# Copies and their subtractions issued apart, and new delays, in a hybrid attention / recurrence layer kernel

## The chip, the core and the metric

The kernel runs on one core of a Trainium2 chip. The metric is the device time of one execution in microseconds (us); several executions are timed and their median is given. Beside them stands one profiled execution, whose trace shows every instruction on five engines: TensorE (PE, with its weight loads as PEld), VectorE (DVE), ScalarE (ACT), GpSimd (POOL) and SyncE (SP, which here only issues DMA transfers, one after the other).

## What is computed

One decoder layer on 512 tokens of width 1024, all in float32. One input projection of width 5912 feeds two mixers: sparse attention (8 heads in 2 groups, with a compressed, a selected-block and a window branch; with 512 tokens the last two both see all earlier tokens) and a gated linear recurrence (4 heads). Each is multiplied by a SiLU gate and projected back; sigmoid gates merge the two; an output projection and a layer norm on `alpha * x + y @ w_out` follow.

```
h = x @ w_in + b_in
q_a, kv_a, g_nsa, z_a, q_b, f_b, i_b, z_b, gm_a, gm_b = split(h)
o_a = nsa_attention(q_a, kv_a, g_nsa) * silu(z_a)
o_b = rmsnorm(hgrn2(q_b, f_b, i_b)) * norm_g * silu(z_b)
y   = sigmoid(gm_a) * (o_a @ w_branch_a) + sigmoid(gm_b) * (o_b @ w_branch_b)
out = layer_norm(alpha * x + y @ w_out)
```

## The kernel before, in words

**Split products.** Every large float32 product is made of three passes in the rounded format float32r: each operand is split into a high part (a copy that rounds, on ACT) and a low part (the operand minus its high part, on DVE), and hi*hi, hi*lo and lo*hi are summed. `split2` (L169) writes the two instructions one behind the other: ACT's copy is L170, DVE's subtraction L171. It is used on the weights (`split`, L231), keys (L576), queries (L586), values (L339), the attention's probabilities (`values`, L728), both mixers' outputs (`ob`, L492, and `oa`, L783) and the merged `y` (L948).

**The projections.** The columns are taken in tiles of 128, in the order `qb0` to `qb3`, then four `proj_i` tiles, then the list `SEQ` (L39), then 16 gate tiles `ga0 gb0 ... gb7`. `proj` (L276) asks for the load of the weight tile three ahead (`load`, L226, a 512 KB transfer into one of three `wraw` buffers), splits the one two ahead, and makes 24 matmuls of 512 columns (8 row blocks, three passes) into a `pa` bank, of which there are two. The result is then moved out of the bank by ACT with its bias.

**The weave.** Everything between the projections is written by generators that a small scheduler in Python, `_Weave` (L74), moves on. `weave.tick()` is called once for every six projection matmuls (in `proj_v`, twelve shorter ones); it resumes each generator whose delay is over; `yield n` asks for n ticks of delay. The delays stand in the dictionary `D` (L70). `claim` keeps users of the same PSUM banks apart. `drain` runs ticks until no generator is left. A later place in this program means a later place in TensorE's queue and in SP's, which keep the order of the program. On ACT, DVE and GpSimd a planner at compile time, with estimated times of its own, chooses among what it takes for ready; earlier in the program goes first. On the chip every engine then takes its queue in order.

**The attention.** `attn_scores` (L645) walks through six units (a block of 128 queries with one or both branches), the longest first. For each it writes score matmuls, then masks and minima (`masked`, DVE L676) with the exps (ACT L679), then `soften` (L686): the reciprocal sums, the scaling by the gates (ACT L700, DVE L702), and transposes of 32x32 blocks into the tile `big` (DVE L710). 16 transfers on SP (L721) carry `big` into `turn`, which completes the transposition; a unit's transfers need the unit before to have left `turn` (`spent`). `values` then splits each part of `turn` (copy, subtraction) and multiplies it with the values. `attn_sum` (L757) adds the branches, multiplies with the gate (L781) and splits the result as `oa`.

**The recurrence.** `hgrn(h)` (L388) runs once per head; `hgrn_norm` (L462) makes the norm. Its four broadcasts (16 transfers) are followed by a product on GpSimd (L488), the gate (L490) and the split into `ob`.

**The end.** Eight branch steps (`BRANCH`, L47, four for mixer b, then four for a, two tiles of `m` each) multiply `ob` and `oa` with the branch weights; L942 and L946 merge, and `y` is split. Meanwhile `out_ahead` (L902) loads the output weights, takes the mean of their rows off (L884, L886) and splits them (L898 on ACT, L899 on DVE). The output product runs over eight row blocks `kt` and needs `y[kt]` and output weight `kt` in turn; its first tile takes both halves of a `kt` together.

Of the kernel before, what the change touches and what calls it, by code (L numbers as in the profile page):

```python
# [18 lines left out]
P = 128  # L19
# [19 lines left out]
SEQ = "kslc q0 kwin q1 v q2 q3 kcmp vcmp zb0 zb1 zb2 zb3 za0 za1 za2 za3".split()  # L39
# [30 lines left out]
D = dict(h0=6, h2=4, h3=7, h4=0, h5=5, h6=3, n0=6, n1=7, n2=4, c0=1, c1=5, c2=5, c3=4, r0=5, p0=5, p1=5, p2=2, s0=8,  # L70
         s2=5, s3=0, v0=10, v1=8, v2=7, v3=8, e0=4, e1=3, t0=6, t1=5, t2=4, t3=5, t4=1, a5=0)
# [35 lines left out]
def layer_kernel(ctx: ExitStack, tc: tile.TileContext, xT, xn, w0, wi, wf, wv, small, brow, consts,  # L107
# [18 lines left out]
    t2 = ctx.enter_context(tc.tile_pool(name="t2", bufs=57))  # L126
# [45 lines left out]


# [64 lines left out]
    for i in range(3):  # L238
        load(i)
# [32 lines left out]
    split(1)  # L272

    weave = _Weave()

    def proj(name):  # L276
        i = M_INDEX[name]
        load(i + 3)
        split(i + 2)
# [36 lines left out]
    def proj_v():  # L316
        i = M_INDEX["v0"]
        load(i + 3)
        split(i + 2)
        load(i + 4)  # L320
        for tt in range(4):
            c = slice(128 * tt, 128 * tt + 128)
            ps = PA()
            for kt in range(KT):
                if kt % 4 == 0:
                    weave.tick()
                if kt < 6:
                    n = slice(PV * (kt % 3), PV * (kt % 3) + NV)
                    hi, lo = (t[:, n] for t in parts[i + kt // 3])
                else:  # L330
                    hi, lo = vtail[kt - 6]
                T.matmul(ps[:, 0:NV], xh[kt][:, c], hi, start=kt == 0, stop=False)
                T.matmul(ps[:, 0:NV], xh[kt][:, c], lo, start=False, stop=False)
                T.matmul(ps[:, 0:NV], xl[kt][:, c], hi, start=False, stop=kt == KT - 1)
            v = T2(NV)
            tc.keep_in_program_order(V.tensor_tensor(v, ps[:, 0:NV], brv, ALU.add))
            vd = vv[:, tt].rearrange("p b (g c) -> p b g c", c=64)
            v4 = v[:, 0:256].rearrange("p (b g c) -> p b g c", b=2, c=64)
            split2(v4, vd[:, :, 0:4:3], vd[:, :, 1:3])  # L339
            G.tensor_copy(gat[:, tt], v[:, 256:NV])  # L340
            vts.append(vv[:, tt])
        gates()
        split(i + 3)
# [8 lines left out]
    def evac(name):  # L352
        ps, m = proj(name)
        r = T2()
        A.activation(r, ps, AF.Identity, bias=bias(m))
        return r
# [105 lines left out]
    def hgrn_norm():  # L462
# [21 lines left out]
        for h in range(4):  # L484
            while "zb%d" % h not in zs:
                yield 1
            o = osq[h][0]
            G.tensor_tensor(o, o, rms[h], ALU.mult)  # L488
# [3 lines left out]
            split2(o, *ob[h])  # L492
            yield 1
# [63 lines left out]
    def gates():  # L557
        gflat = gat.rearrange("p i c -> p (i c)")
        A.activation(gflat, gflat, AF.Exp, scale=-1.0)
        V.tensor_scalar(gflat, gflat, 1.0, 2.0, ALU.add, ALU.mult)  # L560
# [15 lines left out]
    def keys(br, raw):  # L576
        r, rot = rope(raw)
        yield D["r0"]
        V.tensor_tensor(rot, rot, sinT, ALU.mult)
        V.tensor_tensor(r, r, rot, ALU.add)  # L580
        split2(r, KH[:, br], KL[:, br])
        ready.add("keys%d" % br)
# [3 lines left out]
    def queries(m, q):  # L586
# [4 lines left out]
        QAB[m] = T2(dt=F32R), T2(dt=F32R)  # L591
        split2(r, *QAB[m])
# [93 lines left out]
    def soften(u, ms, ts, den):  # L686
        i, brs = units[u]
        n, nb, nm = 128 * (i + 1), len(brs), len(ms)
        while "gates" not in ready:
            yield 1  # L690
# [4 lines left out]
        for ab in range(2):  # L695
            for z, m in enumerate(ms):
                for x in range(nb):
                    c, h = slice(n * x, n * x + n), (ab * nm + z) * nb + x
                    if z % 2:
                        A.mul(ts[m, ab][:, c], ts[m, ab][:, c], den[:, h:h + 1])  # L700
                    else:
                        V.tensor_scalar(ts[m, ab][:, c], ts[m, ab][:, c], den[:, h:h + 1], None, ALU.mult)  # L702
# [25 lines left out]
    def values(u, st, lo):  # L728
# [3 lines left out]
        split2(lo.bitcast(F32), hi, lo)  # L732
# [24 lines left out]
    def attn_sum():  # L757
# [19 lines left out]
        for m in range(4):  # L777
# [4 lines left out]
            oa[m] = T2(dt=F32R), T2(dt=F32R)  # L782
            split2(r, *oa[m])  # L783
            yield 1
# [37 lines left out]
    def cmp_tile(a, name):  # L822
        ps, m = proj(name)
# [3 lines left out]
        weave.start(cmp_hidden(a, de))  # L827
# [3 lines left out]
    def q_tile(m):  # L831
        qraw.append(evac("q%d" % m))
        weave.start(queries(m, qraw[m]))
# [4 lines left out]
    for name in SEQ:  # L838
        if name[1:] == "cmp":
            cmp_tile("kv".index(name[0]), name)  # L840
            if name[0] == "v":
                weave.start(cmp_kv())
            continue
        if name[0] == "k":
            weave.start(keys(int(name == "kwin"), evac(name)))
            continue
        if name[0] == "q":
            m = int(name[1])
            if m == 0:
                split_vtail()  # L850
            q_tile(m)
            if m == 1:
                weave.start(hgrn_norm(), D["s2"])
            if m == 3:
                weave.start(cmp_scores(), D["s3"])
                weave.start(attn_sum())
            continue
        if name == "v":
            weave.start(attn_scores(), D["s0"])
            proj_v()  # L860
            continue
        ps, m = proj(name)
# [4 lines left out]
        V.scalar_tensor_tensor(z, t, 1.0, z, ALU.add, ALU.mult)  # L867
        zs[name] = z
# [12 lines left out]
    def minus_mean(src, scale=1.0):  # L881
        s = SM(2, "rsum")
        for hf in range(2):
            A.activation(src[hf], src[hf], AF.Identity, scale=scale, accum_out=s[:, hf:hf + 1])  # L884
        nm = SM(1, "nm")
# [3 lines left out]
    wmean = {}  # L889

    def mean_out(kt):
        wmean[kt] = minus_mean(woraw[kt])

    def split_out(kt):
        hl = [(T2(dt=F32R), T2(dt=F32R)) for _ in range(2)]
        nm = wmean[kt]
        for raw, (hi, lo) in zip(woraw[kt], hl):
            A.activation(hi, raw, AF.Identity, bias=nm)  # L898
            V.scalar_tensor_tensor(lo, raw, nm, hi.bitcast(F32), ALU.add, ALU.subtract)  # L899
        wo.append(hl)  # L900

    def out_ahead(n):  # L902
        n += AHEAD
        load_out(n + 2)
        if 0 <= n < 8:
            split_out(n)
        if 0 <= n + 1 < 8:
            mean_out(n + 1)


    gm = {}
    for i in range(8):
        for c in "ab":
            name = "g%s%d" % (c, i)
            ps, m = proj(name)
            gm[name] = T2()
            with tc.issue_after(exps[-1]):
                A.activation(gm[name], ps, AF.Tanh, bias=hbias[:, m:m + 1], scale=0.5)
# [3 lines left out]
    y, rb = [], {}  # L922
    lg, lbn = [T2(), T2()], [T2(), T2()]
    for n, (mix, m0) in enumerate(BRANCH):
        i = len(M_TILES) + n
        load(i + 3)
        split(i + 2)
# [3 lines left out]
        for m in (m0, m0 + 1):  # L931
# [9 lines left out]
            r = T2()  # L941
            V.scalar_tensor_tensor(r, gm["g%s%d" % (mix, m)], 1.0, ps, ALU.add, ALU.mult)  # L942
            if mix == "b":
                rb[m] = r
            else:
                V.tensor_tensor(r, r, rb[m], ALU.add)  # L946
                hl = T2(dt=F32R), T2(dt=F32R)
                split2(r, *hl)  # L948
                y.append(hl)
        out_ahead(n)  # L950
    for hf in range(2):
# [8 lines left out]
    for tt in range(4):  # L960
        for hf in range(2):
            dma(res[tt][hf], xn[128 * tt:128 * tt + 128, 512 * hf:512 * hf + 512])
        nm = minus_mean(res[tt], ALPHA)
# [150 lines left out]
```

## Time and profile before

| | |
|---|---|
| time, median of 3 runs | 426.77 us (426.23 to 586.89) |
| the profiled execution's own time | 427.06 us |
| its span, first to last instruction | 425.2 us |
| TensorE / VectorE / ScalarE / GpSimd busy | 409.8 / 314.8 / 239.2 / 10.1 us |
| granted TensorE clock, mean | 0.994 |
| moved by DMA | 58.05 MB |

Times within the trace count from the span's start. In a row of the timeline stand start, duration, engine, line, operation, tiles, shapes, and in brackets the idle time of the engine just before with the instruction that ended it. A row of the waits reads: engine, tile and line that waited, whom it waited for, us in total, how often, the longest. A row of the windows has the length of the stretch, then the busy time and the number of instructions of PE, PEld, DVE, ACT and POOL, then the granted clock, the busy share of the DMA engines and GB/s. A row of the groups has line, engine, operation, tiles, shapes and count, then busy us in all and mean ns of one, then the idle time just before them.

### The profile page before, as it was taken

The page shows a single profiled execution, that of the slowest core. Times are in us where ns is not written, and L with a number is a line of the kernel's source. Part 1 is how long each engine was busy: PE and PEld are TensorE (multiplying, and loading weights), DVE is VectorE, ACT ScalarE, POOL GpSimd, SP SyncE. Part 2 cuts the span into 40 slices and gives each one's busy share as a digit, 9 for nine tenths or more (in the row PEclk, how much of TensorE's full clock was granted, in tenths as well). Part 3 has the DMA queues.
Part 4 walks back from the last instruction along what each step waited for, and adds up shares of the span by engine and source line. Part 5 has one row for each costly group of instructions (what it writes and reads, how often), then busy time and mean ns, then how long its engine had stood idle before and what let it go on. Part 6 is the DMA issues. An engine that isn't in the chain of part 4 may idle for free.

```text
span 425.2 us, 5979 instructions
## 1 busy us (share of the span) xinstructions
PE 409.8 (96%) x2063; PEld 334.2 (79%) x2063; DVE 314.8 (74%) x636; ACT 239.2 (56%) x469; POOL 10.1 (2%) x22
## 2 busy tenths in 40 slices
PE   9999999999999999979999999999999978999994
PEld 8888888889978687757887787788878856887884
DVE  5925698977485979987699679489766699774493
ACT  4535653544476635783667676578584776528301
POOL 2000000000010220000000000000000000000000
PEclk9999999999999999989999999999999999999999
DMA  7995300324113564804821542723944843026022
GB/s 263 396 387 174 137 0 22 130 76 143 57 49 106 170 202 109 256 2 131 206 109 50 132 168 77 190 81 99 230 167 101 293 142 107 0 72 226 2 100 98
DMA packets 25630, 58.05 MB, mean 137 GB/s; under 512 B 4480, under 2 KB 6400, under 8 KB 25600
## 3 DMA queue, kind: packets, MB, share of 16 engines
q1 hardware_dynamic: 25168, 57.28, 43.1%
q10 hardware_dynamic: 432, 0.39, 0.3%
q8 instruction: 16, 0.26, 0.3%
q14 instruction: 14, 0.11, 0.1%
HBM read 41.93 MB, written 2.10 MB: 104 GB/s over the span
## 4 chain that ended last, share of the span: by engine, by line
PE 78%; DVE 8%; ACT 5%; SPq 4%; DMA 2%; issue 2%; DVEq 0%; ACTq 0%
PE pa L115 51%; PE pso L115 12%; PE pss L115 12%; SPq L122 4%; PE pst L115 2%; DMA wraw<-in_wbr_dram 1%; DVE t L171 1%; DVE big L710 1%; ACT t L170 1%; DVE t L942 1%; DVE wlo L171 1%; ACT whi L170 1%; PE pst L119 1%; ACT t L679 1%; DVE t L899 1%
## 5 line engine op out<-in xcount | busy, mean ns | idle before, releaser
L115 PE MATMUL pa<-t,whi 128*128 128x512 f32 x640 | 201.5, 395 | 4.4 <-DVE t L171 3.0
L115 PEld LDWEIGHTS pa<-t,whi 128*128 128x128 f32 x640 | 118.6, 189 | 34.6 <-DVE t L171 4.3
L115 PE MATMUL pa<-t,wlo 128*128 128x512 f32 x320 | 125.0, 391 | 0.0
L171 DVE TENSOR_TENSOR wlo<-wraw,whi 128x1024 fp32r<-128x1024 f32 x46 | 56.7, 1234 | 23.7 <-ACT whi L170 23.6
L115 PEld LDWEIGHTS pa<-t,wlo 128*128 128x128 f32 x320 | 60.2, 188 | 12.8
L170 ACT CAST whi<-wraw 128x1024 fp32r<-128x1024 f32 x46 | 48.1, 1045 | 30.5 <-PE pa L115 24.1
L679 ACT ACTIVATE t<-t,sm_mn 128x512 f32<-128x512 f32 (+3 forms) x64 | 35.2, 551 | 27.6 <-DVE sm_mn L676 27.6
L115 PE MATMUL pso<-t,t 128*128 128x512 f32 (+2 forms) x158 | 32.8, 342 | 0.0
L115 PE MATMUL pss<-t,t 128*128 128x512 f32 (+2 forms) x158 | 30.6, 324 | 0.0
L171 DVE TENSOR_TENSOR turn<-turn,t 128x1024 fp32r<-128x1024 f32 x20 | 23.6, 1215 | 7.3 <-ACT t L170 7.2
L115 PEld LDWEIGHTS pso<-t,t 128*128 128x128 f32 x158 | 25.2, 189 | 3.7
L115 PE MATMUL pa<-t,t 128*128 128x512 f32 (+1 forms) x104 | 27.2, 366 | 0.0
L710 DVE STREAM_TRANSPOSE big<-t 128x512 f32<-128x512 f32 (+2 forms) x48 | 25.8, 590 | 1.0 <-PE pss L115 1.0
L115 PEld LDWEIGHTS pss<-t,t 128*128 128x128 f32 x158 | 24.0, 190 | 2.9
L170 ACT CAST t<-turn 128x1024 fp32r<-128x1024 f32 x20 | 20.0, 1048 | 3.8 <-DMA turn<-big 3.4
L115 PEld LDWEIGHTS pa<-t,t 128*128 128x128 f32 x104 | 18.3, 188 | 3.1
L170 ACT CAST t<-t 128x512 fp32r<-128x512 f32 (+1 forms) x18 | 10.6, 595 | 17.5 <-DVE t L946 12.7
L115 PE MATMUL pa<-turn,t 128*128 128x512 f32 x64 | 19.9, 389 | 0.0
L115 PE MATMUL pss<-t,whi 128*128 128x512 f32 x64 | 19.8, 390 | 0.0
L115 PE MATMUL pso<-t,vv 128*128 128x512 f32 x40 | 16.8, 421 | 2.1 <-ACT t L170 2.1
L700 ACT ACTIVATE t<-t,sm_dn 128x512 f32<-128x512 f32 (+3 forms) x32 | 16.0, 555 | 3.6 <-DVE sm_dn L694 3.5
L676 DVE CUSTOM_DVE_ANT_0 t<-pss,t 128x512 f32<-128x512 f32 (+3 forms) x32 | 14.0, 483 | 5.2 <-PE pss L115 5.2
(198 smaller groups left out, 569.9 us busy)
## 6 DMA issues: line engine op xcount, KB each, us to landing
wraw<-in_wf_dram SPq DMA_DIRECT2D x38, 512.0 KB, 3.6
turn<-big SPq DMA_DIRECT2D x48, 128.0 KB, 2.4
wraw<-in_wbr_dram SPq DMA_DIRECT2D x8, 512.0 KB, 6.0
t<-in_wout_dram SPq DMA_DIRECT2D x16, 256.0 KB, 4.5
t<-t SPq DMA_DIRECT2D x48, 64.0 KB, 2.0
turn<-big SPq DMA_DIRECT2D x32, 96.0 KB, 2.2
t<-in_wi_dram SPq DMA_DIRECT2D x8, 256.0 KB, 6.0
big<-in_w_dram SPq DMA_DIRECT2D x8, 256.0 KB, 5.7
```

What stands on the lines that cost most here:

```text
L115: return tc.keep_in_program_order(nc.tensor.matmul(*a, **k))
L119: return tc.keep_in_program_order(nc.tensor.transpose(*a, **k))
L122: tc.keep_in_program_order(nc.sync.dma_start(o, i))
L170: A.copy(dst_hi, src)
L171: V.tensor_tensor(dst_lo, src, dst_hi.bitcast(F32), ALU.subtract)
L676: V.tensor_tensor_reduce(out=p[:, c], in0=dsts[m, ab][:, c], in1=amask[:, 512 - n:512], op0=ALU.add, op1=ALU.min, scale=-0.125, scalar=3.0e38,
L679: A.activation(p[:, c], p[:, c], AF.Exp, bias=mn[:, h:h + 1], scale=-1.0, accum_out=den[:, h:h + 1])
L700: A.mul(ts[m, ab][:, c], ts[m, ab][:, c], den[:, h:h + 1])
L710: V.transpose(view[:, :, :, 4 * ab + m], ts[m, ab][:, 0:128 * nst].rearrange("p (c b s) -> p c b s", b=4, s=32))
L899: V.scalar_tensor_tensor(lo, raw, nm, hi.bitcast(F32), ALU.add, ALU.subtract)
L942: V.scalar_tensor_tensor(r, gm["g%s%d" % (mix, m)], 1.0, ps, ALU.add, ALU.mult)
```

## The change

- A new generator `split_steps` writes the copy, waits `D["y"]` = 2 ticks, and writes the subtraction. It takes the place of `split2` for keys, queries, values, probabilities, `ob`, `oa` and `y`.
- Weights are split by the generator `weights`: copy one tick after `proj` of the tile two ahead begins (`w0`), subtraction three ticks later (`w1`). Raw weights get a pool of their own, `come`, with 2 buffers (before: 3); the common pool `t2` has 59 buffers (before: 57).
- Evictions of projection tiles are written by generators that start in the next tick (`x0` = 0), the branch merges one tick later (`x1` = 1), instead of straight behind their matmuls.
- `SEQ` begins with `kcmp kslc v q0`, and `kwin` stands behind the queries. `attn_scores` starts after `q1`, with delay 5.
- `masked` keeps the minima only; the exps open `soften`. The scaling writes DVE's part first, then, two ticks later, ACT's.
- The norm product of `hgrn_norm` moves from GpSimd to DVE.
- The output weights' `split_out` becomes a generator: start after 4 ticks (`o2`), sums, 2 ticks (`o0`), mean, 6 ticks (`o1`), copies, 2 ticks, subtractions.
- All `oa` gates are written in one tick; `branch_a` splits each. Behind the branch steps stands a second `weave.drain()`.
- Most delays in `D` have other values.

```
-SEQ = "kslc q0 kwin q1 v q2 q3 kcmp vcmp zb0 zb1 zb2 zb3 za0 za1 za2 za3".split()
+SEQ = "kcmp kslc v q0 q1 q2 q3 kwin vcmp zb0 zb1 zb2 zb3 za0 za1 za2 za3".split()
-D = dict(h0=6, h2=4, h3=7, h4=0, h5=5, h6=3, n0=6, n1=7, n2=4, c0=1, c1=5, c2=5, c3=4, r0=5, p0=5, p1=5, p2=2, s0=8,
-         s2=5, s3=0, v0=10, v1=8, v2=7, v3=8, e0=4, e1=3, t0=6, t1=5, t2=4, t3=5, t4=1, a5=0)
+D = dict(h0=6, h2=5, h3=14, h4=0, h5=7, h6=8, n0=6, n1=3, n2=4, c0=1, c1=3, c2=4, c3=3, r0=5, p0=5, p1=6, p2=2, s0=5,
+         s2=11, s3=2, v0=10, v1=11, v2=5, v3=9, e0=4, e1=2, t0=5, t1=5, t2=4, t3=2, t4=1, a5=1, y=2, w0=1, w1=3,
+         x0=0, x1=1, e2=0, e3=2, o0=2, o1=6, o2=4)
+    come = ctx.enter_context(tc.tile_pool(name="come", bufs=2))
-    t2 = ctx.enter_context(tc.tile_pool(name="t2", bufs=57))
+    t2 = ctx.enter_context(tc.tile_pool(name="t2", bufs=59))
+    def split_steps(src, dst_hi, dst_lo):
+        A.copy(dst_hi, src)
+        yield D["y"]
+        V.tensor_tensor(dst_lo, src, dst_hi.bitcast(F32), ALU.subtract)
-            raws[i] = strm.tile([P, 1024], F32, name="wraw", tag="wraw")
+            raws[i] = come.tile([P, 1024], F32, name="wraw", tag="wraw")
+    def split_later(i):
+        if i < len(order) and i not in parts:
+            weave.start(weights(i), D["w0"])
+    def weights(i):
+        hi = strm.tile([P, 1024], F32R, name="whi", tag="whi")
+        A.copy(hi, raws[i])
+        yield D["w1"]
+        lo = strm.tile([P, 1024], F32R, name="wlo", tag="wlo")
+        V.tensor_tensor(lo, raws[i], hi.bitcast(F32), ALU.subtract)
+        parts[i] = hi, lo
...
-            G.tensor_tensor(o, o, rms[h], ALU.mult)
-            yield 2
+            V.tensor_tensor(o, o, rms[h], ALU.mult)
...
-                                A.activation(p[:, c], p[:, c], AF.Exp, bias=mn[:, h:h + 1], scale=-1.0,
-                                             accum_out=den[:, h:h + 1])
-                weave.start(soften(u, ms, ts, den), D["e1"])
+                weave.start(soften(u, ms, ts, mn, den), D["e2"])
...
     def split_out(kt):
+        s = row_sums(woraw[kt])
+        yield D["o0"]
+        nm = minus_mean(s)
+        yield D["o1"]
         hl = [(T2(dt=F32R), T2(dt=F32R)) for _ in range(2)]
         for raw, (hi, lo) in zip(woraw[kt], hl):
             A.activation(hi, raw, AF.Identity, bias=nm)
+        yield D["y"]
+        for raw, (hi, lo) in zip(woraw[kt], hl):
             V.scalar_tensor_tensor(lo, raw, nm, hi.bitcast(F32), ALU.add, ALU.subtract)
...
-            split_out(n)
+            weave.start(split_out(n), D["o2"])
...
+    def merge(mix, m, ps):
+        r = T2()
+        V.scalar_tensor_tensor(r, gm["g%s%d" % (mix, m)], 1.0, ps, ALU.add, ALU.mult)
+        if mix == "b":
+            rb[m] = r
+            return
+        V.tensor_tensor(r, r, rb[m], ALU.add)
+        yield D["y"]
+        y[m] = T2(dt=F32R), T2(dt=F32R)
+        yield from split_steps(r, *y[m])
+            weave.start(merge(mix, m, ps), D["x1"])
+    weave.drain()
```

More of the change, by code (lines that the diff above doesn't have):

```diff
@@ L236, in split @@
             parts[i] = hi, lo
-    for i in range(3):
+    def split_later(i):
[8 more added lines that the diff above has]
+        parts[i] = hi, lo
+    for i in range(2):
         load(i)
@@ L272, in layer_kernel @@
     split(1)
+    load(2)
     weave = _Weave()
@@ L278, in proj @@
         load(i + 3)
-        split(i + 2)
+        split_later(i + 2)
         hi, lo = parts[i]
@@ L318, in proj_v @@
         load(i + 3)
-        split(i + 2)
-        load(i + 4)
+        split_later(i + 2)
         for tt in range(4):
@@ L334, in proj_v, with values_of @@
                 T.matmul(ps[:, 0:NV], xl[kt][:, c], hi, start=False, stop=kt == KT - 1)
[L335 to L343, printed above, removed]
+            weave.start(values_of(tt, ps), D["x0"])
+            if tt == 1:
+                load(i + 4)
+                split_later(i + 3)
+        weave.start(gates(), 1)
+    def values_of(tt, ps):
+        v = T2(NV)
+        V.tensor_tensor(v, ps[:, 0:NV], brv, ALU.add)
+        yield D["y"]
+        vd = vv[:, tt].rearrange("p b (g c) -> p b g c", c=64)
+        v4 = v[:, 0:256].rearrange("p (b g c) -> p b g c", b=2, c=64)
+        G.tensor_copy(gat[:, tt], v[:, 256:NV])
+        vts.append(vv[:, tt])
+        yield from split_steps(v4, vd[:, :, 0:4:3], vd[:, :, 1:3])
     def silu_tile(name):
@@ L580, in keys @@
         V.tensor_tensor(r, r, rot, ALU.add)
[L581 removed]
+        yield from split_steps(r, KH[:, br], KL[:, br])
         ready.add("keys%d" % br)
@@ L590, in queries @@
         V.tensor_tensor(r, r, rot, ALU.add)
-        QAB[m] = T2(dt=F32R), T2(dt=F32R)
-        split2(r, *QAB[m])
+        qab = T2(dt=F32R), T2(dt=F32R)
+        yield from split_steps(r, *qab)
+        QAB[m] = qab
     PTc = {}
@@ L694, in soften @@
         V.tensor_tensor(den4, den4, gate[:, :, ms[0]:ms[0] + nm], ALU.mult)
[L695 to L702, printed above, removed]
+        for odd in range(2):
+            for ab in range(2):
+                for z, m in enumerate(ms):
+                    for x in range(nb):
+                        c, h = slice(n * x, n * x + n), (ab * nm + z) * nb + x
+                        if z % 2 == odd:
+                            if odd:
+                                A.mul(ts[m, ab][:, c], ts[m, ab][:, c], den[:, h:h + 1])
+                            else:
+                                V.tensor_scalar(ts[m, ab][:, c], ts[m, ab][:, c], den[:, h:h + 1], None, ALU.mult)
+            if odd == 0:
+                yield D["e3"]
         yield D["t0"]
@@ L781, in attn_sum, with branch_a @@
             V.tensor_tensor(r, r, zs["za%d" % m], ALU.mult)
-            oa[m] = T2(dt=F32R), T2(dt=F32R)
-            split2(r, *oa[m])
-            yield 1
+            weave.start(branch_a(m, r), 1)
+    def branch_a(m, r):
+        oa[m] = T2(dt=F32R), T2(dt=F32R)
+        yield from split_steps(r, *oa[m])
     oa = [None] * 4
@@ L826, in cmp_tile, with q_tile, z_tile @@
                      AF.Identity, bias=bias(m))
-        weave.start(cmp_hidden(a, de))
+        yield from cmp_hidden(a, de)
     qraw = []
-    def q_tile(m):
-        qraw.append(evac("q%d" % m))
-        weave.start(queries(m, qraw[m]))
-    for t in range(4):
-        weave.start(hgrn(t), D["h0"])
-        proj_i(t)
[L838 to L862, printed above, removed]
+    def q_tile(m, ps, b):
+        qraw.append(evac(ps, b))
+        yield from queries(m, qraw[m])
+    def z_tile(name, ps, m):
         z, t = T2(), T2()
@@ L866, in layer_kernel, with k_tile @@
             A.activation(t, ps, AF.Tanh, bias=hbias[:, m:m + 1], scale=0.5)
+        yield D["y"]
         V.scalar_tensor_tensor(z, t, 1.0, z, ALU.add, ALU.mult)
         zs[name] = z
+    def k_tile(br, ps, m):
+        yield from keys(br, evac(ps, m))
+    for t in range(4):
+        weave.start(hgrn(t), D["h0"])
+        proj_i(t)
+    for name, after in zip(SEQ, SEQ[1:] + [""]):
+        if after == "v":
+            split_vtail()
+        if name == "v":
+            proj_v()
+            continue
+        ps, m = proj(name)
+        if name[1:] == "cmp":
+            weave.start(cmp_tile("kv".index(name[0]), ps, m), D["x0"])
+            if name[0] == "v":
+                weave.start(cmp_kv())
+        elif name[0] == "k":
+            weave.start(k_tile(int(name == "kwin"), ps, m), D["x0"])
+        elif name[0] == "q":
+            weave.start(q_tile(int(name[1]), ps, m), D["x0"])
+            if name == "q1":
+                weave.start(hgrn_norm(), D["s2"])
+                weave.start(attn_scores(), D["s0"])
+            if name == "q3":
+                weave.start(cmp_scores(), D["s3"])
+                weave.start(attn_sum())
+        else:
+            weave.start(z_tile(name, ps, m), D["x0"])
     wo, woraw = [], {}
@@ L905, in out_ahead, with gate_tile @@
         if 0 <= n < 8:
-            split_out(n)
-        if 0 <= n + 1 < 8:
-            mean_out(n + 1)
+            weave.start(split_out(n), D["o2"])
     gm = {}
+    def gate_tile(name, ps, m):
+        gm[name] = T2()
+        with tc.issue_after(exps[-1]):
+            A.activation(gm[name], ps, AF.Tanh, bias=hbias[:, m:m + 1], scale=0.5)
+        yield 1
     for i in range(8):
@@ L926, in layer_kernel @@
         load(i + 3)
-        split(i + 2)
+        split_later(i + 2)
+        while i not in parts:
+            weave.tick()
         hi, lo = parts[i]
```

52 lines of the change are left out of this document (24 added, 28 removed).

## The prediction

> **What bounds the kernel now.** I read the page's busy line first, then the waits of TensorE alone, then the stretches around each wait, and last the queues that feed it. The busy line and the first full stretch of the chain say that TensorE is the bound.
>
> ```profile
> PE 409.8 (96%) x2063; PEld 334.2 (79%) x2063; DVE 314.8 (74%) x636; ACT 239.2 (56%) x469; POOL 10.1 (2%) x22
> 358.11 2.72 PE pa L115 x12
> ```
>
> Twelve matmuls take 2.72 us, 0.227 us each from start to start, so a step of six (a tick) takes 1.36 us. The change adds and removes no matmul. All it can win is the time in which TensorE stands; here is that time, in full but for the one wait before the first load (1.1 us):
>
> ```profile
> PE pa L115 <- DVE t L171: 3.0, 3, 1.6
> PE pso L115 <- ACT t L170: 2.1, 1, 2.1
> PE pa L115 <- DVE t L942: 1.4, 1, 1.4
> PE pst L115 <- DVE t L171: 1.0, 1, 1.0
> PE pso L115 <- DVE turn L171: 0.8, 1, 0.8
> PE pst L115 <- ACT t L170: 0.7, 1, 0.7
> ```
>
> They sum to 9.0 us and lie at four places, which the timeline of TensorE shows:
>
> ```profile
> 142.55 0.50 PE L115 MATMUL pst<-kh,t 64*128 64x512 f32 x2 [0.99 <-DVE t L171]
> 186.64 0.51 PE L115 MATMUL pso<-t,vv 128*128 128x512 f32 x1 [2.07 <-ACT t L170]
> 187.90 0.50 PE L115 MATMUL pso<-turn,vv 128*128 128x512 f32 x1 [0.75 <-DVE turn L171]
> 188.52 0.63 PE L115 MATMUL pso<-turn,vv 128*128 128x512 f32 x1
> 188.94 0.63 PE L115 MATMUL pso<-t,vv 128*128 128x512 f32 x1
> 348.50 0.70 PE L115 MATMUL pa<-t,whi 128*128 128x512 f32 x2 [1.38 <-DVE t L942]
> 354.60 0.50 PE L115 MATMUL pa<-t,whi 128*128 128x512 f32 x1 [1.56 <-DVE t L171]
> 384.62 1.92 PE L115 MATMUL pst<-t,t 128*128 128x512 f32 x6 [0.68 <-ACT t L170]
> ```
>
> A matmul is shown as busy for about 0.39 us (the wlo row of the page, below) while the next one starts 0.227 after it, so each wait hides 0.16 more. Place 1, the scores of unit 0 for queries 2 and 3: 0.99 + 0.16 = 1.15. Place 2, the first `values` of unit 0: 2.07 + 0.75 + 0.32 = 3.1, and behind it a slow clock: starts are 0.42 apart instead of 0.227 (188.52 to 188.94), over some seven matmuls 1.4 us; together 4.5. Place 3, the first `a` branch product, which needs `oa`: 1.38 + 3.0 + 4 x 0.16 = 5.0. Place 4, the last `y` in the output product: 0.68 + 0.16 = 0.85. In all 11.5 us. The profiled execution took 427.06 (0.3 above the median 426.77), its span 425.2; with all four gone it would be 427.06 - 11.5 = 415.6.
>
> ```profile
> 187.90:191.50 3.60, 3.60 (x9) 2.74 (x10) 3.60 (x5) 2.47 (x3) 0.00 (x0) 0.57 0.00 0
> 346.70:354.60 7.90, 3.51 (x12) 1.65 (x12) 7.90 (x14) 6.93 (x14) 0.00 (x0) 1.00 0.40 134
> ```
>
> The clock column is 0.57 behind place 2 and 1.00 across place 3, though the latter's pauses are longer in sum. So 1.4 us is a price of place 2 only. The Trainium skill (TensorE: Matmul & The Clock Gate, section "Part 1: The HAM clock gate") has the clock halve only after an idle window of about 3.4 us; here pauses of 2.07 and 0.75 with one matmul between sufficed, and the trace decides. By the page a shortened place 2 would leave no clock cost at all, and my sum below would be about 0.4 lower.
>
> **Part by part.** Instructions on DVE and ACT stand in the planner's order, those on TensorE and SP in the order of the program, which the ticks make. I count ticks from the first of `proj_i`.
>
> *Norm product on DVE.* Four GpSimd products go, four DVE products of 0.69 come (as L946): 2.8 us on DVE.
>
> ```profile
> L488 POOL TENSOR_TENSOR t<-t,t 128x512 f32<-128x512 f32 x4 | 5.6, 1391 | 32.7 <-DMA t<-t 32.7
> L946 DVE TENSOR_TENSOR t<-t,t 128x512 f32<-128x512 f32 x8 | 5.5, 691 | 0.2
> 140.66 1.28 POOL L488 TENSOR_TENSOR t<-t,t 128x512 f32<-128x512 f32 x1 [20.42 <-DMA t<-t]
> 140.72 1.77 DVE L171 TENSOR_TENSOR t<-t,t 128x512 fp32r<-128x512 f32 x1
> 146.95 1.84 DVE L171 TENSOR_TENSOR wlo<-wraw,whi 128x1024 fp32r<-128x1024 f32 x1
> 154.63 1.77 DVE L867 SCALAR_TENSOR_TENSOR t<-t,t 128x512 f32<-128x512 f32 x1
> ```
>
> But three DVE instructions that met these products were held: 1.77, 1.84 and 1.77, where L946 takes 0.69, the mean wlo (a row below) 1.23 and an L899 (below), of L867's kind, 0.75. They lost 1.1 + 0.6 + 1.0 = 2.7, so DVE's total stays. The first of them is the very subtraction that place 1 waits for: without its 1.1, that wait is 0.05. Besides, the queries' scores now come 8 ticks after q3's projection (tick 56 after 48; before 54 after 48), 2.7 us more. Against this stand the subtraction's two ticks of delay (`y`=2) and the first scores at tick 47, the same tick in which q1's subtraction is written. Place 1 gains 1.0 (between 0 and 1.15).
>
> *Unit 0's values.* The 16 `turn` transfers are written at tick 68 in both; the first `values` product moves from tick 78 to 80, and eight compressed-score matmuls (about 0.9 us) go ahead of it: TensorE comes 3.6 us later.
>
> ```profile
> L122 SPq DMA_DIRECT2D turn<-big x16: 512/590/597, 164.3 to 173.8; - x16
> L170 ACT CAST t<-turn x4: 1039/1042/1045, 185.5 to 189.3; 128x1024 fp32r<-128x1024 f32 x4
> DMA to landing us min/median/max: 2.3/2.4/2.7
> ```
>
> The data were there at 173.8 + 2.4 = 176.2, and the copy started at 185.5: it stood 9.3 us behind other work in ACT's order, not behind the transfers. So if the copies stay where they are, 3.6 covers the 3.1 and the clock's 1.4; if the planner moves them along by the same two ticks, nothing is won. The transposes too are written 3 ticks later (66, not 63), with 3 fewer ticks to the transfer. I take 3.4 of the 4.5 (0 to 4.5), since the slack of 9.3 is in ACT's queue, where exps now have a step of their own.
>
> *`oa` and the output weights (place 3).* Before, the output weights' copies and subtractions (L898, L899) are written among the steps that lead to `oa`. Now `split_out` waits 4 + 2 + 6 + 2 = 14 ticks, so that the first subtraction is written at tick 166, and all four `oa` subtractions at tick 163; five ticks before TensorE asks.
>
> ```profile
> 335.67 1.05 ACT L170 CAST whi<-wraw 128x1024 fp32r<-128x1024 f32 x1 [2.25 <-DMA wraw<-in_wbr_dram]
> 338.59 1.19 ACT L747 COPY t<-pso 64x512 f32<-64x512 f32 x2
> 353.86 0.68 DVE L171 TENSOR_TENSOR t<-asum,t 128x512 fp32r<-128x512 f32 x1
> L899 DVE SCALAR_TENSOR_TENSOR t<-t,sm_nm,t 128x512 fp32r<-128x512 f32 x16 | 11.5, 748 | 0.6 <-PE pss L115 0.6
> ```
>
> The last `oa` was ready at 353.86 + 0.68 = 354.54. Between 337 and 354, six L899 (4.5 us) stood ahead of it on DVE, and the ACT copy that starts the chain (338.59) stood behind a weight that came late. That weight follows unit 5's transfers, which wait for the last `values` of unit 4, now at tick 145 instead of 148: 4.1 us earlier. So 4.5 + 2 to 4 against a lack of 5.0: I take 4.2 (2 to 5).
>
> *Place 4, what is deferred.* DVE's work up to the last `y` stays the same, and there is little room:
>
> ```profile
> 323.10:346.70 23.60, 23.60 (x105) 19.51 (x104) 16.20 (x23) 14.56 (x26) 0.00 (x0) 1.00 0.64 205
> 354.60:374.40 19.80, 19.80 (x87) 16.38 (x88) 16.93 (x27) 9.36 (x19) 0.00 (x0) 1.00 0.09 28
> 374.40:385.40 11.00, 10.32 (x46) 7.92 (x44) 8.09 (x13) 4.53 (x7) 0.00 (x0) 1.00 0.45 118
> DVE t L171 <- ACT t L170: 4.9, 7, 0.7
> ```
>
> DVE worked 16.20 + 7.90 + 16.93 + 8.09 = 49.1 of 62.3 us from tick 152 to the last `y`. Without places 3 and 4 there are 56.4 us for them. The first window has 7.4 idle, and the deferral leaves three or four more output weights (2 x 0.75 each, 4.5 to 6) for later. What pays for it are the seven waits of 0.7 between a copy and its subtraction (4.9), which `y`=2 fills. Net between -0.85 and +5; I take +1.3.
>
> *Weights.* The raw ring shrinks from 3 to 2, and the subtraction is written 4 ticks before its use instead of 8. The load, once free to run ahead, now waits for the subtraction of the weight before (12 ticks before use), with all later transfers behind it on SP.
>
> ```profile
> wraw<-in_wf_dram SPq DMA_DIRECT2D x38, 512.0 KB, 3.6
> 318.04 10.01 SPq L122 DMA_DIRECT2D turn<-big  x16
> L170 ACT CAST whi<-wraw 128x1024 fp32r<-128x1024 f32 x46 | 48.1, 1045 | 30.5 <-PE pa L115 24.1
> L171 DVE TENSOR_TENSOR wlo<-wraw,whi 128x1024 fp32r<-128x1024 f32 x46 | 56.7, 1234 | 23.7 <-ACT whi L170 23.6
> L115 PE MATMUL pa<-t,wlo 128*128 128x512 f32 x320 | 125.0, 391 | 0.0
> ```
>
> Behind a block of 16 the way is 10.0 + 3.6 + 1.05 + 1.23 = 15.9 us. Twelve ticks are 16.3 at 1.36, and 21.6 at the attention stretch's mean (348.50 - 186.64 over 90 ticks is 1.8). So it is covered by 0.4 to 5.7 us; if that cover is gone each block costs its lateness. I put 1.0 for all (0 to 15).
>
> *The rest.* Evictions are written in the next tick's first step: two `pa` buffers cover one tile (4 ticks, 5.4 us) against an eviction below 0.7, cost 0. SEQ, the exps split from the minima and the scaling by halves move instructions without adding any; the recurrence's delays spread its DVE work. The drain ahead of the `a` products writes five output weights' steps early and issues nothing on TensorE. Together 0, between -1 and +2; I take +0.3, for the first scores.
>
> **Sum.** 427.06 - 1.0 - 3.4 - 4.2 + 1.3 + 1.0 + 0.3 = 421.06; less the 0.3 by which the profiled run lies above the median: about **420.8**. A measurement of this kernel tells some 2% (8.5 us) from no change.
>
> **Rivals.**
>
> *All four places close.* 415.6 - 0.3 = 415.3. For it: in the queue each late thing is late by order, not by work (9.3 us at place 2), and unit 5's chain comes 4 us sooner. Against: DVE would have to be busy for 49.1 of 56.4 us in a stretch that begins with waits.
>
> *The gain is given back.* The planner, not the program, decides where the copies stand; place 2 stays at 4.5, and what place 3 gains comes back before the last `y`: 427.06 - 1.0 + 0.3 - 0.3, some 426. For it: the planner already put L781 between L899s, so handwritten distance may change little. Against: the seven waits of 0.7 show that it doesn't fill all.
>
> *Slower: loads behind blocks.* With two raw buffers SP stands on a load until DVE has done a subtraction, and the block of 16 behind it starts late; the next weight is then late for TensorE. It decides from 5.7 us of lateness in the attention stretch, 0.4 in a stretch of bare ticks. At 3.3 us over that in five of six blocks: 16.5 us on 420.8, less the 1.0 already put, about 436.3. For it: the blocks take 10 us six times and cannot be passed. Against: while TensorE waits, everything else catches up, and the ticks around blocks are the long ones.
>
> **How the numbers follow.** Forecast 0.42 (its own range 417 to 424.5), all four close 0.26, given back 0.20, slower 0.12. Faster by over 2% means under 418.2: all of the second and a tenth of the first, 0.30. Slower by over 2%, above 435.3: most of the last, 0.10. Within 2%: 0.60. The range reaches from 414 (all closed, and one more short wait) to 430, where the last case and its lead-up are left out.
>
> **What would show it.** Right: the waits of TensorE without the `pst` row from L171 and without a pause above 1 us at unit 0's first values, granted clock 1.0 there; the `oa` subtractions before the L899 of output weights 1 to 4; a wait of 1 to 3 us in the output product's first tile. Wrong: rows in which `pa` waits for whi or wlo, or long SP waits on wlo ahead of a block of 16 (the slower rival); the casts of unit 0's `turn` still 9 us after landing (given back).

## The result, and the profile after

The changed kernel takes 421.52 us (median of 6 runs, 420.13 to 424.28), the kernel before 426.85 (6 runs beside it): a ratio of 0.9883 [0.9849, 0.9918], 5.3 us less. The interval lies clear of no change, although the prediction held that only 2% could be told from it. The 586.89 us among the executions of the kernel before belongs to a slow one and stays out of the ratio. The profiled execution took 421.37, its span 419.6, 5.69 less than the profiled 427.06 of before. The forecast of 420.8 is 0.7 from the median. The busy line of the page and TensorE's waits (in total, times, longest):

```profile
PE 408.2 (97%) x2063; PEld 333.9 (80%) x2063; DVE 312.7 (75%) x640; ACT 239.1 (57%) x469; POOL 4.6 (1%) x18
PE pso L116 <- DVE turn L179: 2.0, 1, 2.0
PE pa L116 <- DVE sm_nm L930: 1.5, 1, 1.5
PE pso L116 <- DVE t L189: 1.0, 1, 1.0
PE pso L116 <- ACT t L177: 0.9, 1, 0.9
PE pa L116 <- DVE t L972: 0.3, 1, 0.3
```

Without the wait of the start (L189) 4.8 us are left of 9.0 (2.03, 1.50, 0.92 and 0.34 in the rows below). With the hidden 0.16 for each of the four it is 5.4, where the prediction counted 11.5 with the slow clock. The difference, 6.1, is 0.4 more than what was measured. Of the old waits only 0.34 is left; the other three rows are new or stand elsewhere.

**Unit 0's first values (place 2): the wait is gone.** The timeline of SP, ACT and TensorE there, and the stretch behind it (the column after the engines is the granted clock):

```profile
166.62 10.18 SPq L123 DMA_DIRECT2D turn<-big  x16
178.79 0.72 ACT L718 ACTIVATE t<-t,sm_mn 128x512 f32<-128x512 f32 x1 [2.54 <-DVE sm_mn L702]
179.52 1.99 ACT L177 CAST t<-turn 128x1024 fp32r<-128x1024 f32 x2
188.19 0.40 PE L116 MATMUL pso<-t,vv 128*128 128x512 f32 x1
188.20:191.80 3.60, 3.60 (x17) 2.93 (x16) 3.60 (x8) 3.59 (x5) 0.00 (x0) 1.00 0.00 0
```

The last transfer lands at about 166.62 + 10.18 + 2.4 = 179.2 (2.4 is the median way to landing); the cast starts 0.3 later, where it started 9.3 later in the kernel before. The planner has put it ahead of three of unit 1's four exps. The product starts 6.7 us after the cast has ended, and the clock stays 1.00.

**Unit 1's first values: a wait that was not there.** SP, ACT and TensorE again:

```profile
203.49 11.79 SPq L123 DMA_DIRECT2D turn<-big  x16
218.31 0.62 ACT L718 ACTIVATE t<-t,sm_mn 128x384 f32<-128x384 f32 x1 [2.54 <-DVE sm_mn L702]
222.36 2.92 ACT L177 CAST t<-turn 128x1024 fp32r<-128x1024 f32 x3
223.44 0.50 PE L116 MATMUL pso<-t,vv 128*128 128x512 f32 x1 [0.92 <-ACT t L177]
225.97 0.50 PE L116 MATMUL pso<-turn,vv 128*128 128x512 f32 x1 [2.03 <-DVE turn L179]
```

The data landed at 203.49 + 11.79 + 2.4 = 217.7, the cast started 4.7 later, behind exps of the next unit that had waited 2.54 for their minima. It is the picture of place 2, one unit on.

**`oa` (place 3) and the products behind it.** ACT, DVE and TensorE:

```profile
340.14 2.43 ACT L177 CAST t<-asum 128x512 fp32r<-128x512 f32 x4 [0.56 <-DVE asum L817]
342.97 2.50 DVE L179 TENSOR_TENSOR t<-asum,t 128x512 fp32r<-128x512 f32 x4
347.70 1.41 DVE L943 SCALAR_TENSOR_TENSOR t<-t,sm_nm,t 128x512 fp32r<-128x512 f32 x2
346.20 0.70 PE L116 MATMUL pa<-t,whi 128*128 128x512 f32 x2 [0.34 <-DVE t L972]
358.04 0.68 DVE L972 SCALAR_TENSOR_TENSOR t<-t,pa 128x512 f32<-128x512 f32 x1
358.87 0.71 PE L116 MATMUL pa<-t,whi 128*128 128x512 f32 x2 [1.50 <-DVE sm_nm L930]
```

All four `oa` are ready at 345.47 (354.54 before), ahead of the first deferred subtraction (L943 at 347.70). What had been put off comes next: between 347.70 and 358.04 DVE works through ten L943 among others, and the merge L972 that frees the bank for the next `a` product stands behind them. The 1.50 is put down to the tiny L930; what frees a bank, though, is the L972 in the row above. It ended at 358.72, 0.15 before TensorE went on; at 346.20 the same way took 0.14 (the L972 there ended at 346.06). Without the deferred work in front of it (experiment 8) the wait is gone. No wait is left in the output product.

### The profile page after: what moved, and what is told of

The parts are those of the page before. It is cut to its first block, busy times and chain, and to the rows that moved or that the text cites. A ratio compares the mean times of both kernels' runs of the same rounds, so it can differ in the third digit from the quotient of the medians.

```text
span 419.6 us, 5940 instructions
## 1 busy us (share of the span) xinstructions
PE 408.2 (97%) x2063; PEld 333.9 (80%) x2063; DVE 312.7 (75%) x640; ACT 239.1 (57%) x469; POOL 4.6 (1%) x18
## 4 chain that ended last, share of the span: by engine, by line
PE 84%; DVE 7%; SPq 3%; ACT 3%; DMA 2%; issue 1%; DVEq 0%; ACTq 0%
PE pa L116 55%; PE pso L116 12%; PE pss L116 12%; PE pst L116 5%; SPq L123 3%; ACT t L718 2%; DMA wraw<-in_wbr_dram 2%; DVE big L746 1%; DVE wlo L254 1%; DVE t L943 1%; PE pst L120 1%; DVE asum L788 1%; DVE t L787 1%; DVE t L179 1%; DVE asum L817 1%
## 5 line engine op out<-in xcount | busy, mean ns | idle before, releaser
L254 DVE TENSOR_TENSOR wlo<-wraw,whi 128x1024 fp32r<-128x1024 f32 x44 | 53.6, 1219 | 31.2 <-ACT whi L251 30.2
L251 ACT CAST whi<-wraw 128x1024 fp32r<-128x1024 f32 x44 | 46.1, 1047 | 29.2 <-PE pa L116 19.7
L116 PEld LDWEIGHTS pso<-t,t 128*128 128x128 f32 x158 | 26.1, 197 | 3.9
L116 PE MATMUL pso<-turn,vv 128*128 128x512 f32 x40 | 16.0, 399 | 2.0 <-DVE turn L179 2.0
L177 ACT CAST t<-t 128x512 fp32r<-128x512 f32 x16 | 9.8, 615 | 13.4 <-DVE t L976 11.4
```

Source lines behind the costliest of these rows:

```text
L116: return tc.keep_in_program_order(nc.tensor.matmul(*a, **k))
L177: A.copy(dst_hi, src)
L251: A.copy(hi, raws[i])
L254: V.tensor_tensor(lo, raws[i], hi.bitcast(F32), ALU.subtract)
```

## The experiments

**1. The weights' ring.** Is the two-buffer ring a cost?

```
-    come = ctx.enter_context(tc.tile_pool(name="come", bufs=2))
-    t2 = ctx.enter_context(tc.tile_pool(name="t2", bufs=59))
+    come = ctx.enter_context(tc.tile_pool(name="come", bufs=3))
+    t2 = ctx.enter_context(tc.tile_pool(name="t2", bufs=57))
```

> The changed kernel with three raw weight buffers again (and 57 common ones, as before). My theory: the SP waits on wlo fall from 85.7 us, unit 1's block of 16 starts up to 1.5 us earlier, but the copies of unit 1 stand behind exps on ACT, so the time falls by no more than 1: 420.5 to 421.5. Rival (the smaller ring costs, as the slower rival had it): 2 to 3 us faster, unit 1's waits of 0.92 and 2.03 gone. The other way, two common buffers fewer hold the output weights: up to 1 slower.

423.39 us, ratio 0.9917 [0.9886, 0.9948]. SP's waits on wlo fell, and TensorE's did not; first the row of the changed kernel, then that with three buffers:

```profile
SPq L123 <- DVE wlo L254: 85.7, 16, 12.3
```

```profile
SPq L123 <- DVE wlo L254: 46.0, 7, 12.4
```

No product of TensorE waits for a weight in either, so SP's waiting is not on its path. The changed kernel does show what the prediction named as a sign of the slower rival, a long wait of SP on wlo ahead of a block of 16: 9.9 us, just ahead of unit 1's (203.49). It cost nothing: with three buffers unit 1's block starts at 202.93, and its waits are the same 0.92 and 2.03. The slower rival is out, and so is the 1.0 of the sum. The kernel with three buffers is 1.9 slower (0.9 in the profiled executions), which is not explained in full. Its trace has a wait of 1.2 for an eviction (at 86.88), which the changed kernel does not have, and a slow clock behind unit 1's pause (0.57 from 226 to 230, where the changed kernel has 1.00); with two common buffers fewer besides, the run does not tell what the third buffer alone is worth.

**2. The norm product on VectorE, alone**, in the kernel before (G to V in L488).

> The kernel before, with the norm product alone moved to DVE. My theory: the subtraction at place 1 is no longer held by GpSimd, the pst wait of 0.99 us falls below 0.2, the rest stays: 0.8 to 1.1 us faster, 425.8. Rival (the queries' transfers are what is late): the pst wait stays near 1 us and the time at 426.8. A third: four more DVE products of 0.69 lengthen place 2, 427.5.

427.03, ratio 1.002 [0.9998, 1.0043]. Place 1's wait fell from 0.99 to 0.52, not to 0.05: the subtraction no longer takes 1.77, but the product now stands ahead of it on DVE.

```profile
141.20 0.69 DVE L488 TENSOR_TENSOR t<-t,t 128x512 f32<-128x512 f32 x1
141.81 0.68 DVE L171 TENSOR_TENSOR t<-t,t 128x512 fp32r<-128x512 f32 x1
142.55 0.50 PE L115 MATMUL pst<-kh,t 64*128 64x512 f32 x2 [0.52 <-DVE t L171]
```

The time did not change; the 0.8 to 1.1 us that were expected did not come.

**3. Unit 0's products two ticks later, alone**, in the kernel before. This was the prediction's ground for place 2.

```
-        yield D["t2"]
+        yield D["t2"] + 2 * (u == 0)
```

> The kernel before, with only unit 0's values products two ticks (2.7 us) later, behind copies at the same place. My theory (two ticks of lead are most of place 2's gain): the waits of 2.07 and 0.75 fall to 0 to 0.6 and the clock behind them stays at 1.0: 3 to 4.5 us faster, 423. Rival (the planner moves the copies along): 2 us of wait remain, 426.

434.45, ratio 1.0186 [1.0142, 1.0231]. TensorE waits more, not less:

```profile
PE pso L115 <- ACT t L170: 5.3, 2, 3.6
PE pso L115 <- DVE turn L171: 2.9, 2, 1.8
```

The planner moved the casts along with their consumer. ACT's rows for unit 0 and unit 1:

```profile
187.97 2.95 ACT L170 CAST t<-turn 128x1024 fp32r<-128x1024 f32 x3
229.48 2.92 ACT L170 CAST t<-turn 128x1024 fp32r<-128x1024 f32 x3
```

Unit 0's first cast starts 2.4 later than the 185.54 of before, although its transfers are no later and its place in the program is the same: two activations of another projection now stand ahead of it. Unit 1's stands behind four exps. Unit 0's wait stays and unit 1's comes up. The rival was right about the copies, and the time is slower than either expected; the ground for 3.4 us of the forecast falls.

**4. Unit 1's products two ticks later**, in the changed kernel (with the drain of experiment 8).

> The changed kernel with ticks until the four oa are written in place of the drain ahead of the a products, and unit 1's values products two ticks later. My theory (the 0.92 and 2.03 us at unit 1's first values are a lack of lead, as place 2 was): both go, the clock stays at 1.0, nothing else moves: 417.5 to 419. Rival (the copies follow, or a later unit comes short by the two ticks): 420.5 to 422.

425.03, ratio 0.9969 [0.9954, 0.9985], against 421.19 for the changed kernel with that drain alone: the same again. Unit 1's first cast starts at 227.02 where it started at 222.23 without the two ticks, and its product still waits 1.71 for it. In all 2.1 and 1.9 us of waiting for casts and subtractions stay at units 1 and later, and 2.1 for a `pa` eviction comes on top.

**5. The pairs of `values` taken apart, alone**, in the kernel before; once with the products two ticks later, once at their old ticks (`yield D["t2"] - 2`).

```
-        split2(lo.bitcast(F32), hi, lo)
+        A.copy(hi, lo.bitcast(F32))
+        yield 2
+        V.tensor_tensor(lo, lo.bitcast(F32), hi.bitcast(F32), ALU.subtract)
         yield D["t2"]
```

> The kernel before with one pair alone taken apart: the cast of `turn` and the subtraction behind it in `values`, two ticks between, and the products therefore two ticks later. Separation theory (what the change wins at unit 0's first values is won by the pair being issued apart): TensorE's waits of 2.1 on the cast and 0.75 on the subtraction shrink to under 1 us together, the clock behind them stays 1.0, and the time is 422 to 424.5. Rival (the planner moves the casts along with whatever is written later, as when the products alone were put two ticks later: 434.45): the wait of about 2 us stays at unit 0 or turns up at unit 1, 427 to 434.

> As the run beside it, but the products keep their ticks: cast, two ticks, subtraction, two ticks, product. Separation theory: 423 to 426, with a smaller wait of TensorE at unit 0's first values than the 2.1 + 0.75 before. Rival (order follows the consumer only): within 1 us of before, the casts of unit 0 still some 9 us after the transfers have landed, or slower because the subtraction now has two ticks instead of four to its product.

438.05, ratio 1.0271 [1.0229, 1.0313], and 428.92, ratio 1.0065 [1.0041, 1.0088]. In the second the first wait is the same and the other one longer (1.7 for 0.75):

```profile
PE pso L115 <- ACT t L732: 2.1, 1, 2.1
PE pso L115 <- DVE turn L734: 1.7, 1, 1.7
```

So separating this pair does not close place 2 either; by itself it loses.

**6. The new delays, alone**: the kernel before with the change's values for the delays that it already has.

```
-D = dict(h0=6, h2=4, h3=7, h4=0, h5=5, h6=3, n0=6, n1=7, n2=4, c0=1, c1=5, c2=5, c3=4, r0=5, p0=5, p1=5, p2=2, s0=8,
-         s2=5, s3=0, v0=10, v1=8, v2=7, v3=8, e0=4, e1=3, t0=6, t1=5, t2=4, t3=5, t4=1, a5=0)
+D = dict(h0=6, h2=5, h3=14, h4=0, h5=7, h6=8, n0=6, n1=3, n2=4, c0=1, c1=3, c2=4, c3=3, r0=5, p0=5, p1=6, p2=2, s0=5,
+         s2=11, s3=2, v0=10, v1=11, v2=5, v3=9, e0=4, e1=2, t0=5, t1=5, t2=4, t3=2, t4=1, a5=1)
```

> The kernel before with nothing but the change's values for the delays that it already has: every pair still issued together, the product on GpSimd, three raw buffers, the output weights at their old place. Theory (the step apart and the delays work together: the delays decide which work of the queues stands ahead of unit 0's casts, the steps apart keep the later stages full): in this kernel the casts of unit 0's `turn` stand in ACT's order ahead of the exps of unit 1's second half and ahead of the copy of vcB, so the wait of 2.1 + 0.75 at unit 0's first values goes; but the two waits for `oa` and the wait of the output product stay or grow, since nothing there has changed: 422 to 426. Rival (the delays alone are the gain): 420 to 422.5, as the whole change. Second rival (delays fitted to separated pairs are worth nothing without them): 427 or more, with new waits at units 1 to 5.

449.41, ratio 1.0513 [1.0481, 1.0545]. Here place 2 does close, as rows of ACT, DVE and TensorE show. The cast waits for nothing but the landing (the last transfer had been issued by 178.30), its subtraction ends at 184.12, and the first product waits for nothing at all:

```profile
180.36 1.04 ACT L170 CAST t<-turn 128x1024 fp32r<-128x1024 f32 x1 [2.75 <-DMA turn<-big]
```

```profile
182.94 1.18 DVE L171 TENSOR_TENSOR turn<-turn,t 128x1024 fp32r<-128x1024 f32 x1
```

```profile
194.58 0.50 PE L115 MATMUL pso<-t,vv 128*128 128x512 f32 x1
```

TensorE comes late to it, after the wait of 7.8 below; but this wait ended at 186.53, when the first pair was ready. Other places pay. The kernel's waits of 1 us and more, without the start's:

```profile
PE pst L115 <- DVE t L539: 7.8, 1, 7.8
PE pso L115 <- ACT t L170: 5.5, 2, 5.1
PE pso L115 <- DVE turn L171: 3.1, 3, 1.6
PE pss L115 <- DVE asum L772: 2.9, 1, 2.9
PE pss L115 <- issue: 2.8, 1, 2.8
PE pss L115 <- DVE t L446: 1.1, 1, 1.1
```

The longest, 7.8, is for a copy out of PSUM in the compressed branch (L539), to which DVE came late: ahead of it stood, among others, transposes of unit 1 that waited 4.6 for unit 0's `turn` transfers to have read `big`.

```profile
180.52 1.30 DVE L710 STREAM_TRANSPOSE big<-t 128x512 f32<-128x512 f32 x2 [4.57 <-DMA turn<-big]
186.26 0.21 DVE L539 COPY t<-pst 128x64 f32<-128x64 f32 x1
```

The second rival was right on the time: delays made for separated pairs cost 22 us without them and without the rest of the change. The theory was right on place 2 alone.

**7. The pairs together, with the changed kernel's delays and all else of it.** First with no pause at all (the consumers come two or three ticks earlier), then with the pause behind the subtraction, so that the consumers keep their ticks. The second edit, in `split_steps`; `weights` and `split_out` have the same:

```
         A.copy(dst_hi, src)
-        yield D["y"]
         V.tensor_tensor(dst_lo, src, dst_hi.bitcast(F32), ALU.subtract)
+        yield D["y"]
```

> The changed kernel with every copy and its subtraction written together again (split_steps, weights and split_out without their pauses); order, delays and places stay. My theory: the separation itself is worth little, since the planner fills gaps anyway and DVE's wait for ACT is mostly off the path: within 1 us, 420.5 to 422.5; the seven waits of 0.7 between copy and subtraction of y come back, as 1 us at most in the output product. Rival (the separation is what won): 3 to 5 us slower, 425.

> The changed kernel with copy and subtraction written together, as in the run with the pairs together, but with the pause kept behind the subtraction, so that every product, score and load stands where the change puts it. That run took 443.9, against my theory. Theory one (lead): it lost because the pause also keeps the values' products two ticks behind the transfers, and the weights ready later; with those places kept the time is within 2 us of the changed kernel, 421 to 423.5. Theory two (separation): ACT's and DVE's order is what matters; the time stays near 440, above 432 at least.

443.89, ratio 1.0408 [1.0362, 1.0455], and 429.04, ratio 1.0062 [1.0046, 1.0078]. The first is far slower than either theory expected, the second lies between what its two theories expected. So of the distance to 421.52 the separation itself is 429.04 - 421.52 = 7.5 us, and the ticks that it gives the consumers are another 14.9. The waits of the second kernel:

```profile
PE pso L116 <- DVE turn L178: 2.8, 2, 2.0
PE pst L116 <- ACT t L940: 2.2, 1, 2.2
PE pa L116 <- DVE t L972: 1.2, 2, 0.8
PE pso L116 <- ACT t L177: 0.9, 1, 0.9
PE pst L116 <- DVE t L645: 0.7, 1, 0.7
```

The 2.2 is an output weight's copy in the output product (none in the changed kernel): with the pairs together, the deferral is not paid for. The granted clock adds to the 7.5: it is 0.83 from 380 to 390, behind that wait, which is 1.7 us. As much is lost behind unit 1's pause (0.64 from 226 to 230, 0.93 from 230 to 234), which the changed kernel has as well, though without a slow clock in its profile; so of the 7.2 between the profiled executions (428.57 and 421.37) some 5.5 belong to the separation.

**8. The output weights deferred, alone, in the kernel before; then with the merges as steps.** The first edit is the changed kernel's `split_out` with its four delays and the drain behind the branch products; the second adds its `merge`: sum, two ticks, copy, two ticks, subtraction. A third run leaves the changed kernel as it is, but drains ahead of the `a` products only until `oa` is there:

```
-            weave.drain()
+            while None in oa:
+                weave.tick()
```

> The kernel before, with only the output weights' steps deferred as the change does it (start 4, sums, 2, mean, 6, copies, 2, subtractions, and a drain at the end). My theory (place 3 is L899 and L898 standing ahead of oa): the pa waits of 1.38 and 3.0 at the first a product fall below 1.5 in all, and 1 to 2 us come back at a bank wait of an a product or in the output product: 2 to 3 us faster than before, 424. Rival (the late weight and unit 5's values are what is late): the waits stay above 3 us, the time at 426.

> The kernel before with the output weights deferred (that alone: 429.23, with 3.0 us of waiting for an output weight's copy in the output product and 2.4 for a merge) and the merges of the branch products as steps: sum, two ticks, copy, two ticks, subtraction. Theory (the change can afford the deferral because its merge and its y pair no longer hold DVE behind ACT): both waits fall under 1 us each and the time is 424 to 426. Rival (what pays is the time gained earlier, DVE being free sooner because units 0 to 5 run on time): waits of 3 us or more stay in the output product and the time is 428 to 431.

> The changed kernel, with the drain ahead of the a products replaced by ticks until the four oa are written; the output weights' steps stay spread among the a products. My theory: the 1.50 us wait at the fifth a product (bank held by a merge that stands behind ten L943 on DVE) goes, and no wait as large comes back in the output product: some 1.5 us faster than the changed kernel, 420.0. Rival (DVE's total decides, order doesn't): the wait turns up again as 1 to 2 us in the output product's first tile, 421.5.

Deferred alone: 429.23, ratio 1.0052 [1.0025, 1.008]. With the merges as steps: 424.06, ratio 0.9949 [0.9926, 0.9972]. The changed kernel with the shorter drain: 421.19, ratio 0.9871 [0.9829, 0.9912]. The larger waits of the first from place 3 on, then all of the second there:

```profile
PE pst L115 <- ACT t L899: 3.0, 1, 3.0
PE pa L115 <- DVE t L943: 2.4, 1, 2.4
```

```profile
PE pa L115 <- DVE t L927: 2.1, 1, 2.1
PE pss L115 <- DVE t L927: 0.5, 1, 0.5
```

The deferral takes away place 3 (4.4) and gives 5.4 back: 3.0 in the output product and 2.4 at a bank. With the merges as steps the 3.0 is gone and 2.6 stays at the banks. The medians lie 5.2 us apart, the profiled executions (429.22 and 423.10) 6.1. Of these, 3.0 are the waits of this stage. About 1.7 are the clock behind the wait of 3.0 (0.83 from 380 to 390, against 1.00 in the second kernel), and about 1.6 the clock behind place 2 (0.69 against 0.84 from 184 to 195), which the edit doesn't touch. So some 4.5 come from separate steps in this one stage. What they take out shows in DVE's waits for copies: between 350 and 390 DVE waited 5.7 us, eight times, for the copy in front of a subtraction with the deferral alone, and 0.2 with the merges as steps (before: 4.9, seven times). The expectation had both waits of TensorE under 1, and only one is. The shorter drain removes the wait of 1.5 behind L930 from the changed kernel, and no other comes for it; but 421.19 against 421.52 is within what the intervals leave open, so no version here is shown to beat the change.

## Why the prediction came out right

In profiled executions the stretch terms were forecast at -6.0 in all and came out at -5.7. The total is right through place 3 and through errors that offset one another, which is luck, and one step of it failed.

*Place 1, forecast -1.0: -1.15, but it hung on a tenth of a microsecond.* Neither of the two reasons was needed. In the kernel before, GpSimd's product started 0.06 us ahead of the subtraction (140.66 and 140.72, both shown with the prediction), and the subtraction took 1.77. With the output weights deferred, an edit 200 us further on, the subtraction came first, and it is GpSimd that was held; DVE and GpSimd of that kernel:

```profile
141.48 0.68 DVE L171 TENSOR_TENSOR t<-t,t 128x512 fp32r<-128x512 f32 x1
```

```profile
141.60 1.71 POOL L488 TENSOR_TENSOR t<-t,t 128x512 f32<-128x512 f32 x1 [20.82 <-DMA t<-t]
```

Its wait at place 1 is gone as well, with the product still on GpSimd and the scores at their old tick; so it is in the kernel of experiment 3. In both kernels the one that started first was not held, and the other was: the subtraction 1.77 for 0.68, the product 1.71 for 1.28. In the changed kernel there is room besides: the subtraction ends at 141.14, the scores begin at 142.62.

*Place 2, forecast -3.4: the step that failed.* "TensorE comes 3.6 us later" was taken to cover the wait "if the copies stay where they are"; the doubt was put beside it and priced, but the wrong value was chosen. TensorE did come 3.6 later (188.19 for 186.64 - 2.07). But the copies do not stay: experiments 3 and 4 moved the consumer, and the casts followed. Unit 0 gained all 4.5 mainly because ACT's order changed: the cast starts 6.0 earlier than before (179.52 for 185.54), and the first subtraction ends near 184.7, about when TensorE would have come without the extra ticks. With the delays alone the cast stands early in ACT's order too (experiment 6). And the same kind of wait came up at unit 1, 0.92 + 2.03 + 0.32 = 3.3 of it. Net -1.2, and this with a clock of 1.00 behind unit 1: where it slowed there, in the kernel of the last section, the same pauses cost 1.7 more, and place 2 would have won nothing. The prediction looked at unit 0 alone, while the delays that it weighed hold for six units.

*Place 3, forecast -4.2: -4.5, for the first of the two reasons given.* The order on DVE is as described, `oa` first, and the deferral alone removes these waits (experiment 8), so the second, unit 4's `values` coming earlier, was not needed.

*Place 4, forecast +1.3: +0.8, in another place.* The output product lost its 0.85, and 1.66 turned up at the fifth tile of the `a` products, since the drain writes the deferred work exactly there. The payer named, the pause that fills the waits between a copy and its subtraction, is borne out by experiment 8, where these waits of DVE fall from 5.7 to 0.2.

*Weights, forecast +1.0: 0* (experiment 1). SP's waiting is not on the path while the next weight is there in time.

-1.15 - 1.2 - 4.5 + 0.8 = -6.05, and some 0.4 for all else, against +0.3 forecast for the rest: -5.7. Place 2 fell short by 2.2, and the weights (1.0), place 4 (0.5), place 3 (0.3) and place 1 (0.15) came out better by 2.0.

What no forecast had: how the parts hang together. Delays alone +22.1 (449.41 for 427.35), the changed kernel with its pairs written together again +7.5, one pair apart alone +2.6 to +11.7, the change as a whole -5.3. One part, the norm product, changed nothing; the deferral alone cost 2.8 and won 2.3 with the merges as steps. What inside the planner puts the casts ahead of unit 1's exps with one set of delays and behind them with another was not settled; the runs show only that delays do it and that two ticks on the consumer do not.

## What to carry to other kernels

With a planner that orders a queue, a tick more between producer and consumer need not be slack: the planner may spend it on something else, as it did twice here, so ask of each handwritten distance what will now be put into it, and look at the next unit for the wait that leaves this one. Work put off has to be paid for in the stage that it is put into; here the separate copies and subtractions of the merges were what paid. A set of delays belongs to one way of cutting the steps: of the parts of this change that were tried one by one, none won and most lost.

## What the runs showed of the hardware

The same pause was followed by a slow clock in one kernel and not in the other. The changed kernel and that with the shorter drain have the same waits at unit 1 (0.9 and 2.0). The stretches, first of the changed kernel, then of the other:

```profile
223.00:230.00 7.00, 4.53 (x20) 3.29 (x21) 7.00 (x9) 5.32 (x7) 0.00 (x0) 1.00 0.00 0
```

```profile
226.00:230.00 4.00, 4.00 (x12) 2.87 (x13) 4.00 (x4) 2.09 (x3) 0.00 (x0) 0.64 0.00 0
230.00:234.00 4.00, 4.00 (x20) 3.30 (x19) 2.38 (x4) 1.16 (x2) 0.00 (x0) 0.93 0.58 167
```

4 x 0.36 + 4 x 0.07 = 1.7 us of full speed are lost in the second. The kernel with three buffers and that with the pairs together at their old ticks, which have the same two waits at unit 1, show a slow clock as well (0.57 and 0.64 from 226 to 230). The Trainium skill (TensorE: Matmul & The Clock Gate, section "Part 1: The HAM clock gate") puts the slowing after an idle window of about 3.4 us. The first kernel's trace agrees; the second's, with two pauses of 2.9 in sum and a product between them, does not. The six executions of the changed kernel differ too: the one with a mean clock of 0.989 has a span of 422.5, the others, at 0.993 to 1.000, have 418.3 to 420.1. So a short pause is best priced with a chance of its clock cost, not with the whole of it or nothing.
